# A hybrid-mixer encoder layer in one launch: the recurrence's places moved into the projections' input, its first stage moved ahead of the gated attention's last two heads

## The chip, the cores and the metric

The kernel runs on one core of a Trainium2 chip. The metric is the device time of one execution in microseconds (us). The engines are TensorE (PE, matrix products), VectorE (DVE), ScalarE (ACT), GpSimd (POOL) and SyncE (SP, which only starts DMAs here). Each engine works through its own list of instructions in a fixed order; semaphores hold an instruction back until what it needs is there. "Clock" is the TensorE clock that the profile shows as granted, as a share of full speed.

## The reference, cut to what matters

One encoder layer runs over 768 tokens (a sequence of 512 and one of 256) of 1,024 channels: a hybrid mixer, cross attention to 256 memory rows per sequence, and a feed-forward network. Only the mixer and the key and value product of the memory rows are touched by the change.

```python
def hybrid_mixer(h, p):
    proj = h @ p['w_in']
    rw = centred_shift(proj[..., :R_COLS], p['mu_prev'], p['mu_next'])
    gl = proj[..., R_COLS:]
    mixed = jnp.concatenate([rwkv7_group(rw, p), gla_group(gl, p)], axis=-1)
    return mixed @ p['w_out']

# rwkv7_group: 8 heads of 64, once forward and once in reverse over the tokens
def step(S, inp):
    r_t, w_t, k_t, v_t, kk_t, a_t = inp
    sa = jnp.einsum('bhij,bhj->bhi', S, -kk_t)
    S = (S * w_t[:, :, None, :] + sa[..., None] * (kk_t * a_t)[:, :, None, :]
         + v_t[..., None] * k_t[:, :, None, :])
    return S, jnp.einsum('bhij,bhj->bhi', S, r_t)

# gla_group: 4 heads of gated linear attention in chunks of 64 tokens, both directions
# cross_attention: kv = rms_norm(mem) @ p['wkv_x']
```

## The kernel before, in words

Channels stand on the partitions and tokens on the free axis. A float32 product is made from two rounded halves of each operand (hi and lo) in three matmuls, so a weight tile is loaded, rounded on ACT (`whi`) and its remainder taken on POOL or DVE (`wlo`).

**Projections.** `hT_hi` and `hT_lo` (pool `hp`) hold the normalised input. `blocks([(g, i), ...])` runs projection blocks of 128 columns each: g 0 to 3 are the gated attention's q/k, gate, value and decay columns, g 4, 5 and 6 are the columns r, k and v of the recurrence's head pairs 1, 2 and 3. Their matmuls write `pd` and read `hT_hi` and `hT_lo`.

**The recurrence** handles four pairs of heads, p = 0 to 3. For a pair, `begin(p)` makes decays and products of them on DVE and POOL, and `lower` multiplies them into chunk matrices on PE, which go out by DMA; `invert(p)` reads them back and inverts 96 triangles of 32x32 in a loop of 31 pairs of DVE operations (tiles `stmp`, `sqf`, `snf`); `joined(p)` reads the result by DMA and merges the triangles into 64x64 on PE (tiles `merge`, two passes of 48 matmuls each). The state is then carried over the chunks of 64 tokens by `step`: a chain PE, ACT, PE, ACT, PE, DVE for each pair of chunks, in `stage(q)`. A stage advances up to three independent jobs: the second half of pair q-1's long sequence, and both the first half of it and the short sequence for pair q. What a step reads stands in six "places" of 10 KB a partition (`pl`), filled by `products` from DRAM and PE. `finish` normalises a pair's result.

**The gated attention** runs head by head, `gla_head(h)`, in one arena of 13 x 768 floats (39 KB a partition) in pool `gp`, and ends with a multiply and a DMA to `mixd`.

**The memory rows.** `memory()` loads and splits the normalised memory rows into `mem_hi` and `mem_lo` (32 KB a partition together), and `memory_block(mem, b)`, 16 of them with 48 matmuls of 128x256 each, makes the keys and values. These blocks depend on nothing of the recurrence, so the scheduler lays them between the stages' small matmuls. Then `out_projection` (tiles `po`) multiplies the mixed result by `w_out`, whose hi and lo planes are loaded into tiles that are free by then.

**What sets the order.** The functions are called in program order; `tc.high_priority(offset=...)` draws steps (4000), products (3000), preparation and inversion (2000) and joins (6000) ahead of the calls around them. A scheduler then fixes each engine's list. Space is the other thing: a tile that takes another's place can be written only when the last reader of the old one is done. Around the change the calls before are

```python
        joined(1)
        blocks([(5, i) for i in range(3)])
        gla_head(2)
        blocks([(3, 3), (2, 3)])
        begin(2)
        invert(2)
        gla_head(3)          # pool gp closes; the places open in its space
```

and after these `prods(0, ...)`, `blocks([(6, i) ...])`, `stage(0)`; pool `hp` closes, `memory()` opens in new space, then `begin(3)`, `joined(2)`, `invert(3)`, the 16 memory blocks and stages 1 to 4.

Of the kernel before, what the change touches and what calls it, by code (L numbers as in the profile page):

```python
# [8 lines left out]
F32 = mybir.dt.float32  # L9
F32R = mybir.dt.float32r  # L10
# [6 lines left out]
P = 128  # L17
# [15 lines left out]
def kernel(ctx: ExitStack, tc: tile.TileContext, I, y_prompt, y_sample):  # L33
# [28 lines left out]
    cp = ctx.enter_context(tc.tile_pool(name="cp", bufs=1, reuse_waits="tile"))  # L62
    hp_cm = tc.tile_pool(name="hp", bufs=1, side="right", reuse_waits="tile")
    hp = hp_cm.__enter__()
    wp_cm = tc.tile_pool(name="wp", bufs=2, reuse_waits="tile")
    wp = wp_cm.__enter__()
    dp = ctx.enter_context(tc.tile_pool(name="dp", bufs=1, space=DRAM))
# [377 lines left out]

    def rkv_early(p, i):

        ot = hp.tile([P, T], F32, tag="gd", bufs=2, name="gd")
        rkv_block(p, i, lambda c, n: ot[:, c:c + n])
        dma(rkvd[p, i], ot)  # L450
        if i == 2:
            vt = tokens_first(ot)
            for h, hs in enumerate(HS):
                for par, ps_ in enumerate(HS):
                    dma(vtd[p][h][:, :, par * 64:par * 64 + 64], vt[ps_, :, hs])

    def tokens_first(ot):

        vt = hp.tile([P, T], F32, tag="gd", bufs=2, name="gd")
        for c, n in SEQS:  # L460
            pt = psd("gvt")
            for j in range(0, n, P):
                pe.transpose(out=pt[:, j:j + P], in_=ot[:, c + j:c + j + P], identity=ident)
            with tc.high_priority():
                dve.tensor_copy(out=vt[:, c:c + n], in_=pt[:, 0:n])
        return vt.rearrange("p (j e) -> p j e", e=P)

    def gla_dense(g, i):

        c0 = (1952, 2208, 2992, 2464)[g] + i * P  # L470
        w = load_block([(w_cols(c0, P), 0)], P)
        ot = hp.tile([P, T], F32, tag="gd", bufs=2, name="gd")
# [130 lines left out]

    mp_cm = tc.tile_pool(name="mp", bufs=1, reuse_waits="tile")
    mp = mp_cm.__enter__()
    tts, tdz = [], []
    for d in range(2):
        t = mp.tile([P, NCH, 64], F32, tag=f"tt{d}", name=f"tt{d}")
        pool.memset(t, 0.0)
        tts.append(t)  # L610
        tdz.append(mp.tile([P, NCH, 32], F32, name=f"tdz{d}"))
    px = mp.tile([P, NCH, 66], F32, tag="px", name="px")
    pool.memset(px, 1.0)
    px_at = px[:, :, 1:65]
# [199 lines left out]
    joined(0)  # L814


    with tc.tile_pool(name="gp", bufs=1, reuse_waits="tile") as gp:
        ones_f = gp.tile([P, P], F32, name="ones_f")
        dve.memset(ones_f, 1.0)
        arena = gp.tile([P, 13 * T], F32, name="arena")  # L820
# [119 lines left out]
        blocks([(0, 1), (1, 1), (3, 2), (2, 2)])  # L940
        joined(1)
        blocks([(5, i) for i in range(3)])
        gla_head(2)
        blocks([(3, 3), (2, 3)])
        begin(2)
        invert(2)
        gla_head(3)


    places = {}  # L950

    def open_places(pool_, gs):
        for g in gs:
            t = pool_.tile([P, 2560], F32, tag=f"pl{g}", name=f"pl{g}")
            places[g] = (t[:, 0:512].rearrange("p (h u x) -> p h u x", h=2, x=64),
                         t[:, 512:1280].rearrange("p (u i x) -> p u i x", u=4, x=64),
                         t[:, 1280:1792].rearrange("p (u h x) -> p u h x", u=4, x=64),
                         t[:, 1792:2304].rearrange("p (u x) -> p u x", x=P),
                         t[:, 2304:2560].rearrange("p (u x) -> p u x", x=64))

    mq1_cm = tc.tile_pool(name="mq1", bufs=1, reuse_waits="tile")
    mq1 = mq1_cm.__enter__()
    open_places(mq1, (0, 4, 1, 5, 2))
    yas = [mq1.tile([P, T], F32, tag="ya0", name="ya0")]

    def bc2(ap):

# [39 lines left out]
    def step(st, x, j, pc):  # L1007
# [54 lines left out]
        else:  # L1062
            dve.tensor_tensor(out=o, in0=y1, in1=o, op=ALU.add)
            dve.tensor_tensor(out=o, in0=y2, in1=o, op=ALU.add)

    def finish(st, seqs=SEQS, tiles=None, mixed=None):

        p, pa = st["p"], st["ya"]
        pb, bon, gt = tiles or (mq2.tile([P, T], F32, tag="fb", name="fb"),) * 3
        a, b = seqs[0][0], seqs[-1][0] + seqs[-1][1]  # L1070
        a, b = min(a, seqs[-1][0]), max(b, seqs[0][0] + seqs[0][1])
        cs = slice(a, b)
# [77 lines left out]
                prods(q + 1, (j // 2, 4 + j // 2))  # L1150

    prods(0, (0, 4, 1, 5))
    blocks([(6, i) for i in range(3)])
    stage(0)
    prods(0, (2,))
    hp_cm.__exit__(None, None, None)
    mq2_cm = tc.tile_pool(name="mq2", bufs=1, reuse_waits="tile")
    mq2 = mq2_cm.__enter__()
    open_places(mq2, (3,))
    yas += [mq2.tile([P, T], F32, name=f"ya{i}") for i in (1, 2)]  # L1160
    prods(0, (3,))
    mem = memory()
    begin(3)
    joined(2)
    invert(3)
    for b in range(16):
        memory_block(mem, b)
    stage(1)
    with tc.high_priority(offset=2000):
        finish(sts[0])  # L1170
# [16 lines left out]
    tiles = (mq2.tile([P, T], F32, tag="fb", name="fb"), *mo)  # L1187
# [5 lines left out]
    mq2_cm.__exit__(None, None, None)  # L1193
    hp_cm = tc.tile_pool(name="hp2", bufs=1, side="right", reuse_waits="tile")
    hp = hp_cm.__enter__()
    for k in order:
        if k != 3:
            load_split(mixd[k], *mix[k], lo_eng=pool)
    planes = []
# [8 lines left out]
    planes += [t[:, i, :] for i in range(5)]  # L1208
    wt = {}
    for i, k in enumerate(order):  # L1210
        pl = planes[4 * i:4 * i + 4]
# [77 lines left out]
    with tc.tile_pool(name="op1", bufs=1, reuse_waits="tile") as op1:  # L1289
        g_pre = gain_row(op1, "g_x_pre")  # L1290

        xn = [[op1.tile([P, 512], F32, name="xn")], [t[:, 512:T] for t in mo]]
        mo = [t[:, 0:512] for t in mo]

        def rows():
            return ((rk.tile([P, T], F32, tag="k", name="res0")[:, 0:512], mq1.tile([P, T], F32, tag="ya0", name="res1")[:, 0:512]), mo, xn)

        hT_hi, hT_lo = out_projection(op1, wt, mix, x_rows, rows, g_post, x1d, g_pre)
    mq1_cm.__exit__(None, None, None)
    mp_cm.__exit__(None, None, None)  # L1300
    rk_cm.__exit__(None, None, None)

# [440 lines left out]
```

## Time and profile before

| what | us |
|---|---|
| runs (median; lowest and highest of 3) | 1591.46; 1590.47 to 1599.93 |
| the profiled execution | 1596.87 |
| its span in the profile | 1595.0 |
| PE busy in it | 1442.8 (90%) |
| DVE busy in it | 1049.7 (66%) |
| ACT, POOL busy in it | 718.9, 514.6 |
| mean granted clock | 0.914 |

The profiled execution lies 1.87 us above its span and 5.41 above the median of the runs. Times in the profile count from the start of the span. From 0 to 289 us lie the first projections and the pairs 0 and 1 up to pair 0's join; from 289 to 893 all that the change moves; from 893 on cross attention and the feed-forward network, which it leaves as they are. [...]

### The profile page before, as it was taken

The page shows a single profiled execution, that of the slowest core. Times are in us where ns is not written, and L with a number is a line of the kernel's source. Part 1 is how long each engine was busy: PE and PEld are TensorE (multiplying, and loading weights), DVE is VectorE, ACT ScalarE, POOL GpSimd, SP SyncE. Part 2 cuts the span into 40 slices and gives each one's busy share as a digit, 9 for nine tenths or more (in the row PEclk, how much of TensorE's full clock was granted, in tenths as well). Part 3 has the DMA queues.
Part 4 walks back from the last instruction along what each step waited for, and adds up shares of the span by engine and source line. Part 5 has one row for each costly group of instructions (what it writes and reads, how often), then busy time and mean ns, then how long its engine had stood idle before and what let it go on. Part 6 is the DMA issues. An engine that isn't in the chain of part 4 may idle for free. (4 is left out here: it accounts for less than half of the span.)

```text
span 1595.0 us, 28271 instructions
## 1 busy us (share of the span) xinstructions
PE 1442.8 (90%) x10614; PEld 1246.0 (78%) x10614; DVE 1049.7 (66%) x1605; ACT 718.9 (45%) x1417; POOL 514.6 (32%) x576
## 2 busy tenths in 40 slices
PE   7999689889887889899888999996999999999996
PEld 6887578777775777778767888786999999787785
DVE  5545885497577795764455434448876676878886
ACT  5754344443333332333344354434555556544442
POOL 6416643494317342211531354420000001231223
PEclk9999798989875988888979999997999999999998
DMA  6686555556468447754452333235555447564434
GB/s 168 181 302 188 167 137 131 145 146 192 111 205 229 127 149 176 205 134 135 126 166 99 119 95 105 73 111 160 172 169 176 158 145 284 171 204 132 143 100 142
DMA packets 279565, 250.35 MB, mean 157 GB/s; under 512 B 89264, under 2 KB 227059, under 8 KB 279428
## 3 DMA queue, kind: packets, MB, share of 16 engines
q1 hardware_dynamic: 279428, 248.54, 52.1%
q8 instruction: 84, 1.38, 0.4%
q14 instruction: 53, 0.43, 0.1%
HBM read 164.11 MB, written 82.58 MB: 155 GB/s over the span
## 5 line engine op out<-in xcount | busy, mean ns | idle before, releaser
L148 POOL TENSOR_TENSOR wlo<-wraw,whi 128x256 fp32r<-128x256 f32 x192 | 176.8, 934 | 331.0 <-ACT whi L147 231.1
L247 PE MATMUL pd<-hT_hi,whi 128*128 128x256 f32 (+1 forms) x512 | 182.0, 356 | 12.6 <-DVE gd L325 8.2
L247 PE MATMUL pd<-hT_hi,wlo 128*128 128x512 f32 (+1 forms) x512 | 180.1, 354 | 4.0 <-POOL wlo L148 4.0
L247 PE MATMUL pd<-hT_lo,whi 128*128 128x256 f32 (+1 forms) x512 | 178.6, 350 | 0.3 <-DVE hT_lo L206 0.3
L1511 POOL TENSOR_TENSOR wl<-w,wh 128x1024 fp32r<-128x1024 f32 x8 | 21.2, 2649 | 329.8 <-ACT wh L1510 329.8
L247 PEld LDWEIGHTS pd<-hT_hi,whi 128*128 128x128 f32 x512 | 100.4, 196 | 27.6 <-issue 5.5
L247 PEld LDWEIGHTS pd<-hT_hi,wlo 128*128 128x128 f32 x512 | 99.6, 195 | 18.6 <-POOL wlo L148 5.3
L147 ACT ACTIVATE whi<-wraw 128x256 fp32r<-128x256 f32 x192 | 77.3, 414 | 78.2 <-PE pd L1104 22.9
L247 PEld LDWEIGHTS pd<-hT_lo,whi 128*128 128x128 f32 x512 | 100.4, 196 | 13.0 <-DVE hT_lo L206 0.5
L148 DVE TENSOR_TENSOR ul<-ur,uh 128x768 fp32r<-128x768 f32 x56 | 77.4, 1388 | 30.7 <-ACT uh L147 17.7
L147 ACT ACTIVATE uh<-ur 128x768 fp32r<-128x768 f32 x56 | 47.4, 847 | 107.8 <-PE gz L1520 52.0
L1510 ACT ACTIVATE wh<-w 128x1024 fp32r<-128x1024 f32 x64 | 67.1, 1053 | 35.9 <-PE fz L1520 24.2
L1520 PE MATMUL gx<-wh,uh 128*128 128x512 f32 x192 | 75.0, 397 | 4.3 <-DVE acc L1713 4.3
L1511 DVE TENSOR_TENSOR wl<-w,wh 128x1024 fp32r<-128x1024 f32 x56 | 68.2, 1219 | 15.1 <-ACT wh L1510 14.5
L1520 PE MATMUL gx<-wl,uh 128*128 128x512 f32 x192 | 75.9, 395 | 0.0
L1520 PE MATMUL gx<-wh,ul 128*128 128x512 f32 x192 | 75.4, 395 | 0.0
L1520 PE MATMUL fz<-hh,wh 128*128 128x384 f32 x192 | 66.0, 344 | 1.9 <-ACT wh L1510 1.9
L1511 POOL TENSOR_TENSOR wl<-ws,wh 128x1024 fp32r<-128x1024 f32 x16 | 40.6, 2536 | 79.6 <-ACT wh L1510 79.6
L1520 PE MATMUL fz<-hh,wl 128*128 128x384 f32 x192 | 65.2, 344 | 0.8 <-DVE wl L1511 0.8
L1520 PE MATMUL fz<-hl,wh 128*128 128x384 f32 x192 | 65.8, 343 | 0.0
L1510 ACT ACTIVATE wh<-ws 128x1024 fp32r<-128x1024 f32 x48 | 50.5, 1052 | 26.8 <-PE fx L1520 22.3
L1104 PE MATMUL pd<-mem_hi,whi 128*128 128x256 f32 x256 | 59.3, 308 | 1.4 <-ACT mo L1116 1.4
(476 smaller groups left out, 4306.9 us busy)
## 6 DMA issues: line engine op xcount, KB each, us to landing
w<-in_w_ff_dram SPq DMA_DIRECT2D x64, 512.0 KB
ur<-ud SPq DMA_DIRECT2D x56, 384.0 KB
wraw<-in_w_in_dram SPq DMA_DIRECT2D x108, 128.0 KB
ud<-u SPq DMA_DIRECT2D x32, 384.0 KB
ud<-us SPq DMA_DIRECT2D x24, 384.0 KB
wraw<-in_wkv_x_dram SPq DMA_DIRECT2D x64, 128.0 KB
lora<-lo_t SPq DMA_DIRECT2D x20, 384.0 KB
bkg<-bkd SPq DMA_DIRECT2D x24, 256.0 KB
```

The lines of the kernel that those rows point to most:

```text
L147: act.activation(out=hi, in_=src, func=AF.Copy)
L148: (lo_eng or pool).tensor_tensor(out=lo, in0=src, in1=hi, op=ALU.subtract)
L247: pe.matmul(out=out, lhsT=a, rhs=b, start=(i == 0), stop=(i == n - 1))
L1104: prev = order_after(pe.matmul(out=pd[:, c0:c0 + 256], lhsT=x, rhs=y[:, c0:c0 + 256], start=(k + i + c0 == 0), stop=(k + i + c0 == KD + 25 ...
L1510: act.activation(out=hi, in_=t[name], func=AF.Copy)
L1511: lo_eng.tensor_tensor(out=lo, in0=t[name], in1=hi, op=ALU.subtract)
L1520: pe.matmul(out=out, lhsT=a, rhs=b, start=first and i == 0, stop=last and i == n - 1, skip_group_check=True)
```

## The change

The two buffers `gd` get a pool of their own (`gdp`), which is used again later for two of the results `ya`, and for `xn` and `res1`. The two `tdz` become halves of one tagged tile. Pool `gp` with the arena stays open until after `gla_head(3)`, and four of the six places, with most of a fifth, take the space of `hT_hi` and `hT_lo`, so they can open as soon as the last projection block has read those. All projection blocks now come first, then stage 0, then heads 2 and 3 of the gated attention with the preparation and inversion of pair 2. `mem_hi` and `mem_lo` take the arena's space. Of the planes for `w_out`, 18 take the space of `mem_hi` and `mem_lo` after the last memory block. Nothing is computed that wasn't before, and nothing less.

```diff
-        ot = hp.tile([P, T], F32, tag="gd", bufs=2, name="gd")
+        ot = gdp.tile([P, T], F32, tag="gd", bufs=2, name="gd")
...
-    with tc.tile_pool(name="gp", bufs=1, reuse_waits="tile") as gp:
+    gp_cm = tc.tile_pool(name="gp", bufs=1, reuse_waits="tile")
+    gp = gp_cm.__enter__()
...
         joined(1)
         blocks([(5, i) for i in range(3)])
-        gla_head(2)
         blocks([(3, 3), (2, 3)])
-        begin(2)
-        invert(2)
-        gla_head(3)
+        blocks([(6, i) for i in range(3)])
...
-    mq1_cm = tc.tile_pool(name="mq1", bufs=1, reuse_waits="tile")
+    mq1_cm = tc.tile_pool(name="mq1", bufs=1, side="right", reuse_waits="tile")
     mq1 = mq1_cm.__enter__()
-    open_places(mq1, (0, 4, 1, 5, 2))
-    yas = [mq1.tile([P, T], F32, tag="ya0", name="ya0")]
...
+    plh, pll = (hp.tile([P, KD * T], F32, tag=n, name="pl_" + n) for n in ("hh", "hl"))
+    for t, gs in ((plh, (0, 4)), (pll, (1, 5))):
+        for i, g in enumerate(gs):
+            whole_place(g, t[:, 2560 * i:2560 * i + 2560])
+    place(3, plh[:, 5120:5632], pll[:, 5120:5888], mq1.tile([P, 512], F32, tag="pl3", name="pl3"), plh[:, 5632:6144],
+          pll[:, 5888:6144])
+    whole_place(2, mq1.tile([P, 2560], F32, tag="pl2", name="pl2"))
+    yas = [gdp.tile([P, T], F32, tag="gd", bufs=2, name=f"ya{i}") for i in range(2)]
...
     prods(0, (0, 4, 1, 5))
-    blocks([(6, i) for i in range(3)])
     stage(0)
-    prods(0, (2,))
-    hp_cm.__exit__(None, None, None)
+    prods(0, (2, 3))
+    gla_head(2)
+    begin(2)
+    invert(2)
+    gla_head(3)
+    gp_cm.__exit__(None, None, None)
     mq2_cm = tc.tile_pool(name="mq2", bufs=1, reuse_waits="tile")
     mq2 = mq2_cm.__enter__()
-    open_places(mq2, (3,))
-    yas += [mq2.tile([P, T], F32, name=f"ya{i}") for i in (1, 2)]
-    prods(0, (3,))
     mem = memory()
     begin(3)
     joined(2)
     invert(3)
+    yas.append(mp.tile([P, T], F32, tag="kds", name="ya2"))
     for b in range(16):
         memory_block(mem, b)
+    mq2_cm.__exit__(None, None, None)
     stage(1)
...
+    wo1_cm = tc.tile_pool(name="wo1", bufs=1, reuse_waits="tile")
+    wo1 = wo1_cm.__enter__()
+    planes = [wo1.tile([P, 512], F32R, name=f"w_out{i}") for i in range(18)]
     for n in ("snf", "sqf"):
         t = mp.tile([P, 2, 512], F32R, tag=n, name="w_" + n)
         planes += [t[:, 0, :], t[:, 1, :]]
-    for g in (0, 4, 1, 5):
-        t = mq1.tile([P, 5, 512], F32R, tag=f"pl{g}", name=f"w_pl{g}")
-        planes += [t[:, i, :] for i in range(5)]
+    planes.append(mp.tile([P, T], F32R, tag="tdz", name="w_tdz")[:, 0:512])
```

How the engines' lists move shows in three places. First, the end of the gated attention. On PE before, head 3's last matmuls (`gsum`) stand among the projection blocks (`pd<-hT`):

```order
L247 MATMUL pd<-hT_hi,wlo 128x256
L247 MATMUL pd<-hT_hi,whi 128x256
L921 MATMUL gsum<-arena,ones_f 128x512
L921 MATMUL gsum<-arena,ones_f 128x256
L247 MATMUL pd<-hT_lo,whi 128x256
L247 MATMUL pd<-hT_hi,wlo 128x256
L247 MATMUL pd<-hT_hi,whi 128x256
```

On PE after, they stand behind the last merges of pair 2 and among steps of stage 1 (`rec`); no projection block is left there:

```order
L918 MATMUL go<-arena 128x64 x2
L920 MATMUL go<-arena 128x128
L803 MATMUL merge_5696<-tt_1482,sqf 32x32 x24
L1032 MATMUL rec<-pl_4232 64x64 x4
L1040 MATMUL rec<-rh,pl_4232 64x64 x4
L1027 MATMUL rec<-pl_hh 64x64 x8
L926 MATMUL gsum<-arena,ones_f 128x512
L926 MATMUL gsum<-arena,ones_f 128x256
L1047 MATMUL rec<-pl_4232 64x64 x4
```

Of the two heads' DVE work, what stood beside pair 1's preparation and inversion now stands beside pair 2's inversion and pair 3's preparation.

Second, the first memory block (`pd<-mem_hi`). On PE before, it stands among the products of stage 0 (`sca`, `scb`) and the chunk matrices of pair 2 (`low`), 349 matmuls behind the last projection matmul:

```order
L1049 MATMUL rec<-pl_4468 64x64 x4
L991 MATMUL sca<-pl_4467,bkg 64x64
L992 MATMUL scb<-pl_4467,bkg 64x64
L685 MATMUL low<-bk 64x64
L1104 MATMUL pd<-mem_hi,whi 128x256 x2
L1104 MATMUL pd<-mem_lo,whi 128x256 x2
L685 MATMUL low<-bk 64x64 x14
```

On PE after, it stands in the middle of stage 1, 829 matmuls behind the last projection matmul, and behind pair 2's join:

```order
L1040 MATMUL rec<-rh,pl_hh 64x64 x4
L1032 MATMUL rec<-pl_hh 64x64 x4
L1040 MATMUL rec<-rh,pl_hh 64x64 x4
L1058 MATMUL rec<-pl_4232 64x64 x4
L1116 MATMUL pd<-mem_hi,whi 128x256 x2
L1116 MATMUL pd<-mem_lo,whi 128x256 x2
L1047 MATMUL rec<-pl_hh 64x64 x8
```

All of stage 0, two of four rounds of steps of stage 1, both heads of the gated attention, and pair 2's chunk matrices and join now come before any memory block.

Third, the end of the stages. On PE before, no memory matmul is left when the last steps run, and the output projection (`po`) follows them:

```order
L631 MATMUL hsum<-fb,ones_bd 128x256
L1018 MATMUL rec<-pl_5344 64x64 x4
L1023 MATMUL rec<-pl_5344 64x64 x4
L1031 MATMUL rec<-rh,pl_5344 64x64 x4
L1038 MATMUL rec<-pl_5344 64x64 x4
L1049 MATMUL rec<-pl_5344 64x64 x4
L247 MATMUL po<-w_snf,mix_bk 128x512 x2
```

On PE after, 264 memory matmuls stand between the last step and the output projection. Their beginning:

```order
L1116 MATMUL pd<-mem_hi,wlo 128x256 x2
L1058 MATMUL rec<-pl_hh 64x64 x4
L1125 MATMUL kvt<-ident,mo 128x128 x4
L1116 MATMUL pd<-mem_hi,whi 128x256 x2
L1116 MATMUL pd<-mem_lo,whi 128x256 x2
```

More of the change, by code (lines that the diff above doesn't have):

```diff
@@ L64 @@
     hp = hp_cm.__enter__()
+    gdp_cm = tc.tile_pool(name="gdp", bufs=1, side="right", reuse_waits="tile")
+    gdp = gdp_cm.__enter__()
     wp_cm = tc.tile_pool(name="wp", bufs=2, reuse_waits="tile")
@@ L457, in tokens_first @@
     def tokens_first(ot):
-        vt = hp.tile([P, T], F32, tag="gd", bufs=2, name="gd")
+        vt = gdp.tile([P, T], F32, tag="gd", bufs=2, name="gd")
         for c, n in SEQS:
@@ L471, in gla_dense @@
         w = load_block([(w_cols(c0, P), 0)], P)
-        ot = hp.tile([P, T], F32, tag="gd", bufs=2, name="gd")
+        ot = gdp.tile([P, T], F32, tag="gd", bufs=2, name="gd")
         for c, n, pd in channels_product(w, P, hT_hi, hT_lo):
@@ L605 @@
     mp = mp_cm.__enter__()
-    tts, tdz = [], []
+    tdz = mp.tile([P, 2, NCH, 32], F32, tag="tdz", name="tdz")
+    tdz = [tdz[:, d] for d in range(2)]
+    tts = []
     for d in range(2):
@@ L610 @@
         tts.append(t)
-        tdz.append(mp.tile([P, NCH, 32], F32, name=f"tdz{d}"))
     px = mp.tile([P, NCH, 66], F32, tag="px", name="px")
@@ L814 @@
     joined(0)
-    with tc.tile_pool(name="gp", bufs=1, reuse_waits="tile") as gp:
+    gp_cm = tc.tile_pool(name="gp", bufs=1, reuse_waits="tile")
+    gp = gp_cm.__enter__()
+    if True:
         ones_f = gp.tile([P, P], F32, name="ones_f")
@@ L942, with place, whole_place @@
         blocks([(5, i) for i in range(3)])
-        gla_head(2)
         blocks([(3, 3), (2, 3)])
-        begin(2)
-        invert(2)
-        gla_head(3)
+        blocks([(6, i) for i in range(3)])
     places = {}
[L952 to L959, printed above, removed]
-    mq1_cm = tc.tile_pool(name="mq1", bufs=1, reuse_waits="tile")
-    mq1 = mq1_cm.__enter__()
-    open_places(mq1, (0, 4, 1, 5, 2))
-    yas = [mq1.tile([P, T], F32, tag="ya0", name="ya0")]
+    mq1_cm = tc.tile_pool(name="mq1", bufs=1, side="right", reuse_waits="tile")
+    mq1 = mq1_cm.__enter__()
+    def place(g, xv, a_, bkt, rbk, tp):
+        places[g] = (xv.rearrange("p (h u x) -> p h u x", h=2, x=64), a_.rearrange("p (u i x) -> p u i x", u=4, x=64),
+                     bkt.rearrange("p (u h x) -> p u h x", u=4, x=64), rbk.rearrange("p (u x) -> p u x", x=P),
+                     tp.rearrange("p (u x) -> p u x", x=64))
+    def whole_place(g, t):
+        place(g, *(t[:, a:b] for a, b in ((0, 512), (512, 1280), (1280, 1792), (1792, 2304), (2304, 2560))))
+    plh, pll = (hp.tile([P, KD * T], F32, tag=n, name="pl_" + n) for n in ("hh", "hl"))
[6 more added lines that the diff above has]
+    yas = [gdp.tile([P, T], F32, tag="gd", bufs=2, name=f"ya{i}") for i in range(2)]
     def bc2(ap):
@@ L1064, in step, with finish_tile @@
             dve.tensor_tensor(out=o, in0=y2, in1=o, op=ALU.add)
+    def finish_tile():
+        return mp.tile([P, D], F32, tag="sxf", name="fb")[:, 0:T]
     def finish(st, seqs=SEQS, tiles=None, mixed=None):
         p, pa = st["p"], st["ya"]
-        pb, bon, gt = tiles or (mq2.tile([P, T], F32, tag="fb", name="fb"),) * 3
+        pb, bon, gt = tiles or (finish_tile(),) * 3
         a, b = seqs[0][0], seqs[-1][0] + seqs[-1][1]
@@ L1186 @@
     mo = [mp.tile([P, T], F32, tag="lsb", bufs=4, name="mo") for _ in range(2)]
-    tiles = (mq2.tile([P, T], F32, tag="fb", name="fb"), *mo)
+    tiles = (finish_tile(), *mo)
     with tc.high_priority(offset=2000):
@@ L1192 @@
         finish(sts[3], SEQS[:1], tiles, mix[3])
-    mq2_cm.__exit__(None, None, None)
-    hp_cm = tc.tile_pool(name="hp2", bufs=1, side="right", reuse_waits="tile")
-    hp = hp_cm.__enter__()
     for k in order:
@@ L1198 @@
             load_split(mixd[k], *mix[k], lo_eng=pool)
-    planes = []
+    wo1_cm = tc.tile_pool(name="wo1", bufs=1, reuse_waits="tile")
+    wo1 = wo1_cm.__enter__()
+    planes = [wo1.tile([P, 512], F32R, name=f"w_out{i}") for i in range(18)]
     for n in ("snf", "sqf"):
@@ L1208 @@
     planes += [t[:, i, :] for i in range(5)]
+    planes.append(mq1.tile([P, 512], F32R, tag="pl3", name="w_pl3"))
     wt = {}
@@ L1290 @@
         g_pre = gain_row(op1, "g_x_pre")
-        xn = [[op1.tile([P, 512], F32, name="xn")], [t[:, 512:T] for t in mo]]
+        xn = [[gdp.tile([P, T], F32, tag="gd", bufs=2, name="xn")[:, 0:512]], [t[:, 512:T] for t in mo]]
         mo = [t[:, 0:512] for t in mo]
         def rows():
-            return ((rk.tile([P, T], F32, tag="k", name="res0")[:, 0:512], mq1.tile([P, T], F32, tag="ya0", name="res1")[:, 0:512]), mo, xn)
+            return ((rk.tile([P, T], F32, tag="k", name="res0")[:, 0:512], gdp.tile([P, T], F32, tag="gd", bufs=2, name="res1")[:, 0:512]), mo, xn)
         hT_hi, hT_lo = out_projection(op1, wt, mix, x_rows, rows, g_post, x1d, g_pre)
+    wo1_cm.__exit__(None, None, None)
     mq1_cm.__exit__(None, None, None)
+    gdp_cm.__exit__(None, None, None)
     mp_cm.__exit__(None, None, None)
```

## The prediction

> **What bounds the kernel now.** I read the page, then the windows view (busy time of each engine between two moments), and last the instructions of single tiles and lines. The page:
>
> ```profile
> span 1595.0 us, 28271 instructions
> PE 1442.8 (90%) x10614; PEld 1246.0 (78%) x10614; DVE 1049.7 (66%) x1605; ACT 718.9 (45%) x1417; POOL 514.6 (32%) x576
> ```
>
> PE is the busiest engine on average, but the change touches only a part, cut here at events that the rows further down give: pair 0's join (289), last projection matmul (442), first memory matmul (503), end of pair 2's inversion (607) and of its join (rounded up to 646), last memory matmul (790), last step (826), end of the output projection (rounded to 894). Columns: stretch, length, then busy time of PE, weight load, DVE, ACT and POOL, the granted clock, DMA share and GB/s.
>
> ```profile
> 289.00:442.00 153.00, 136.00 (x1007) 114.96 (x1006) 109.43 (x142) 64.39 (x116) 80.29 (x68) 0.88 0.56 152
> 442.00:503.00 61.00, 46.27 (x649) 37.57 (x648) 46.74 (x87) 24.34 (x68) 24.04 (x22) 0.67 0.75 215
> 503.00:607.00 104.00, 89.35 (x1086) 76.34 (x1087) 87.03 (x182) 33.88 (x92) 49.55 (x41) 0.80 0.55 155
> 607.00:646.00 39.00, 37.55 (x561) 32.30 (x558) 15.92 (x34) 13.02 (x33) 7.29 (x10) 0.97 0.84 200
> 646.00:703.00 57.00, 48.81 (x659) 42.21 (x650) 50.55 (x141) 21.04 (x59) 11.40 (x15) 0.91 0.58 160
> 703.00:790.00 87.00, 84.85 (x1137) 72.58 (x1137) 35.71 (x96) 34.46 (x93) 22.53 (x35) 0.86 0.46 126
> 790.00:826.00 36.00, 25.30 (x178) 18.26 (x178) 24.85 (x56) 17.34 (x48) 16.09 (x26) 0.72 0.64 194
> 826.00:894.00 68.00, 63.58 (x290) 50.66 (x291) 33.12 (x56) 23.60 (x62) 12.13 (x24) 0.97 0.31 100
> ```
>
> Two things are to be seen. Where PE has filler it is nearly full (607 to 646: 37.55 of 39, clock 0.97); where it has only the recurrence's small matmuls (442 to 503) it is busy 46.27 of 61 at a clock of 0.67. And where PE is not full, DVE is: 87.03 of 104 between 503 and 607. PE's work in full-clock microseconds is busy time by clock, row by row: 119.7 + 31.0 + 71.5 + 36.4 + 44.4 + 73.0 + 18.2 + 61.7 = 456. The change keeps these 456 and DVE's work, so the question is only how the pieces cover one another.
>
> **The change, piece by piece.** I follow three stretches: A to the last projection matmul, B to the first memory matmul, C to the output projection.
>
> ```profile
> 289.00:442.00 153.00, 31.18 (x236) 27.22 (x236) 31.11 (x22) 32.87 (x45) 11.31 (x14) 0.88 0.56 152
> L247 PE MATMUL pd<-hT_hi,wlo x144: 274/389/792, 305.7 to 442.2; 128*128 128x512 f32 x72, 128*128 128x256 f32 x72
> L744 DVE TENSOR_TENSOR stmp<-sqf,snf x31: 192/387/925, 377.6 to 415.7; 112x31 f32<-112x31 f32 x2, 112x60 f32<-112x60 f32 x2, 112x87 f32<-112x87 f32 x2, 112x112 f32<-112x112 f32 x2
> L788 PE MATMUL merge<-tdz,lsb x96: 191/191/212, 430.2 to 436.3; 32*32 32x32 f32 x96
> L904 DVE TENSOR_TENSOR_SCAN arena<-arena x2: 3703/3703/3703, 334.4 to 405.8; 64x1536 f32<-64x1536 f32 x2
> L903 DVE TENSOR_TENSOR_SCAN arena<-arena x2: 3350/3390/3431, 331.0 to 402.5; 64x1536 f32<-64x1536 f32 x2
> ```
>
> *A.* The first row is the arena's share of 289 to 442: heads 2 and 3 leave with up to 31.1 us on DVE and 31.2 on PE. Pair 1's join (430.2) stands in PE's list before the last projection matmuls (442.2), 12 us dense, so PE's surplus gives nothing until the join comes earlier. What delays it for certain is in the inversion's loop (377.6 to 415.7): head 3's two scans of 3.4 and 3.7 us, and two multiplications, some 9.5 us. If every DVE microsecond of the heads lay on that chain it would be 31. POOL is busy 80.29 of 153, and pair 1's preparation there stays. I take 10: A ends at 432 instead of 442 (bounds 411 and 442).
>
> ```profile
> L744 DVE TENSOR_TENSOR stmp<-sqf,snf x31: 192/376/1642, 527.6 to 606.5; 112x31 f32<-112x31 f32 x2, 112x60 f32<-112x60 f32 x2, 112x87 f32<-112x87 f32 x2, 112x112 f32<-112x112 f32 x2
> 526.00:609.00 83.00, 76.79 (x165) 0.82 0.44 131
> L800 PE MATMUL merge<-tt,sqf x96: 191/191/212, 630.6 to 636.3; 32*32 32x32 f32 x96
> L1104 PE MATMUL pd<-mem_hi,whi x256: 274/281/581, 503.0 to 789.3; 128*128 128x256 f32 x128
> L147 ACT ACTIVATE mem_hi<-raw x16: 400/402/417, 484.9 to 501.9; 128x256 fp32r<-128x256 f32 x16
> L1019 ACT ACTIVATE rh<-rec x12: 271/278/296, 530.9 to 589.7; 128x128 f32<-128x128 f32 x12
> ```
>
> *B.* Memory tiles take the arena's space, so the first memory matmul waits for head 3's end, and in PE's list it stands behind pair 2's join. In before that chain ran from 442.2: inversion from 527.6 (85 us later) to 606.7, last merge at 636.3. Preparing pair 2 beside stage 0 is the same work as before; it starts a little before the last projection block now and memory's loads are gone from it, so 78 (bounds 66, the 85 less the DVE idle of 442 to 503, and 90). The inversion's 79 us were full of DVE work (second row, DVE alone: 76.79 of 83). Of that, half of stage 1's twelve steps leave (last row: all twelve lay between 530.9 and 589.7), and the two heads come in; leaving and coming nearly cancel at 79 (bounds 65, with every gap closed, and 105, with 31 us of the heads on top). The join's DMAs and merges keep 30. Then head 3's last multiply, its DMA out, and memory's load and split: the 16 splits took 17 us to the first matmul, begun early in part, so 14 (8 to 28). 432 + 78 + 79 + 30 + 14 = 633, where it was 503.0.
>
> Steps on PE now run beside the heads' matmuls and nothing dense. The waits that the change adds are memory's on the arena (SP's loads of the memory rows and their splits on ACT and POOL are queued behind it, then all 16 blocks) and `w_out`'s on the last memory block. The place loads' wait on `hT` costs one DMA trip, in the 78.
>
> ```profile
> L1019 ACT ACTIVATE rh<-rec x11: 270/278/278, 664.8 to 715.6; 128x128 f32<-128x128 f32 x11
> L1019 ACT ACTIVATE rh<-rec x8: 271/278/283, 745.2 to 777.5; 128x128 f32<-128x128 f32 x8
> L1019 ACT ACTIVATE rh<-rec x4: 259/278/278, 781.1 to 816.3; 128x128 f32<-128x128 f32 x4
> 787.42 0.40 PE L1104 MATMUL pd<-mem_hi,wlo 128*128 128x256 f32 x2
> 787.66 0.40 PE L1104 MATMUL pd<-mem_hi,whi 128*128 128x256 f32 x2
> 808.41 1.19 PE L247 MATMUL po<-w_snf,mix_bk 128*128 128x512 f32 x2 [1.29 <-POOL mix_px L148]
> 816.15 0.40 PE L247 MATMUL po<-w_snf,mix_bk 128*128 128x512 f32 x1
> 816.38 1.08 PE L247 MATMUL po<-w_pl,mix_bk 128*128 128x512 f32 x4
> 893.00 0.39 PE L247 MATMUL pd<-hT_hi,whi 128*128 128x512 f32 x1
> ```
>
> *C.* At 633 two rounds of stage 1, four each of stages 2 and 3, and stage 4 are left. One `rh` marks one step: 50.8 us for ten intervals, 32.3 for seven, so 4.6 to 5.1 a step and 14.5 a round of three: 145 for ten rounds. Stage 4 takes 45 (781.1 to 826). Then 264 memory matmuls, two of them each 0.24 us: 31. Sum 221, if the steps never wait for pair 3's join. The other way to reckon is PE: of the 456, A keeps 119.7 less 31.18 x 0.88, thus 92; B gets those 27, the 31 of stage 0, and an estimated 25 of the 108 between 503 and 646 (what its 365 memory matmuls, 43 us, leave is 65, and some two fifths of it, the join, half of stage 1 and pair 2's matrices, come ahead of memory), thus 83; the 288 output projection matmuls at 0.235 are 68. That leaves C 213. At the rate of 646 to 790, 117.4 in 144, it takes (213 - 31) / 0.815 + 31 = 254; at 0.97 it takes 220. I take 230, nearer the steps, since memory covers all of C: the output projection begins at 863, not 808.4.
>
> It took 84.6 (808.4 to 893.0) with the last steps inside; alone 68 / 0.97 = 70, and I add 8 for `w_out` planes that now load after the last memory block (0 to 20). 863 + 78 = 941 against 893.0: **48 us slower**. From the profiled execution, 1596.9 + 48 = 1645; it lay 5.4 above the runs' median, so on that scale 1639.
>
> **The clock.** The row of 442 to 503 has 0.67 where matmuls are sparse, and B is some 200 us of that kind. [...]
>
> **The rivals.**
> - *PE itself sets B.* [...] For it: 442 to 503 is already at 46 of 61 busy. Against it: pair 2's chain is mostly DVE and DMA. [...] Chance 0.14.
> - *Pair 2's inversion runs as pair 1's did.* The same 31 rounds took 38 us at 377.6, beside head 3. Then 41 less: 1598, no change. Against it: pair 3's preparation and both heads stand beside it. Chance 0.17.
> - *Faster: the heads fill DVE's gaps.* DVE's work from 289 to B's end is about 259 (109.43 + 46.74 + 87.03 + 15.92) less 15 for steps that move behind; my A and B give it 344 us, a share of 0.71. At 0.925, its share between 526 and 609, it takes 264, the first memory matmul comes at 560 in place of 633 with the splits, and the time is 1566. It decides from a share of 0.82 (296 us, break-even) and gives over 1% at 0.87. For it: nothing but DVE is full there. Against it: the join's trip (15.92 of 39 busy) and places' loads are DMA waits. Chance 0.13.
> - *The change does not do what it says*: the last projections end no earlier and stage 0 starts as before. Its sum is 10 more, 1649, within my case.
>
> **How the numbers follow.** My forecast has 0.56, 1639, by itself 1612 to 1670 (A's 10 either way, the inversion's 65 and C's 254). The range must reach the no-change case and leaves out the faster one and some large sums of upper bounds: 1588 to 1675. One per cent, 16 us, is what a measurement here can tell. Faster 0.13; same 0.18 (the second rival and a little); slower 0.69.
>
> **What would show it.** Right: last projection matmul near 432; no memory matmul before 615; clock below 0.7 in B; DVE's share from 289 to there near 0.7; a tail of memory matmuls of 31 us at full clock; the output projection from 850 to 880. Wrong: pair 2's inversion under 50 us, memory beginning before 580, or steps in C under 4.5 us apart.

## The result, and the profile after

The changed kernel takes 1696.81 us (median of 4 runs, 1693.43 to 1698.81) against 1593.98 us for the kernel before: a ratio of 1.0639, 95% interval 1.0598 to 1.0679. It is slower, as forecast, by about twice the forecast amount (some 102 us, where 48 had been reckoned), and it lies above the forecast range of 1588 to 1675.

The page of the changed kernel, its first lines:

```profile
span 1696.0 us, 28319 instructions
PE 1464.0 (86%) x10614; PEld 1260.7 (74%) x10614; DVE 1050.6 (62%) x1605; ACT 722.2 (43%) x1417; POOL 495.9 (29%) x576
```

PE, DVE, ACT and POOL run as many instructions as before, and their busy times differ by some 21 us at most; the span has grown by 101. The windows view shows where. The stretches are cut at the changed kernel's own events (columns as in the prediction: length, busy PE, weight load, DVE, ACT, POOL, granted clock, DMA share, GB/s).

```profile
291.50:432.00 140.50, 114.55 (x834) 95.56 (x834) 80.41 (x128) 39.90 (x82) 56.87 (x54) 0.90 0.61 162
432.00:523.00 91.00, 63.95 (x723) 50.89 (x720) 56.77 (x98) 21.38 (x56) 19.12 (x12) 0.55 0.61 163
523.00:600.00 77.00, 44.52 (x356) 35.28 (x356) 71.77 (x105) 26.88 (x42) 29.58 (x28) 0.52 0.29 88
600.00:632.00 32.00, 24.01 (x275) 21.11 (x278) 16.15 (x17) 10.46 (x18) 0.00 (x0) 0.50 0.65 136
632.00:660.00 28.00, 16.85 (x216) 13.47 (x213) 26.36 (x60) 14.28 (x41) 15.61 (x18) 0.56 0.42 119
660.00:707.00 47.00, 38.83 (x613) 32.86 (x617) 31.65 (x89) 12.94 (x39) 6.01 (x8) 0.64 0.48 111
707.00:858.00 151.00, 149.56 (x2012) 126.43 (x2003) 75.94 (x216) 64.67 (x183) 31.25 (x41) 1.00 0.44 130
858.00:890.00 32.00, 29.50 (x241) 28.12 (x240) 3.94 (x5) 12.90 (x27) 16.55 (x26) 1.00 0.46 141
890.00:1000.00 110.00, 82.40 (x375) 66.26 (x374) 50.08 (x87) 39.30 (x101) 32.47 (x61) 0.88 0.39 121
```

From 432 to 660 PE is busy 149 us of 228 at a clock of 0.50 to 0.56, some 80 us of full-clock work. From 707 to 858 it is full (149.56 of 151) at full clock (1.00). The memory matmuls, which ran from 503 on before, now begin at 660 and lie in the later stretch. The events, from the tile view of the changed kernel (first and last start of each group):

```profile
L249 PE MATMUL pd<-hT_hi,wlo x178: 274/390/793, 284.6 to 431.7; 128*128 128x256 f32 x90, 128*128 128x512 f32 x88
L749 DVE TENSOR_TENSOR sqf<-sqf,stmp x31: 192/375/1903, 523.2 to 599.4; 112x31 f32<-112x31 f32 x2, 112x60 f32<-112x60 f32 x2, 112x87 f32<-112x87 f32 x2, 112x112 f32<-112x112 f32 x2
L803 PE MATMUL merge<-tt,sqf x96: 236/236/258, 623.5 to 631.3; 32*32 32x32 f32 x96
L41 SPq DMA_DIRECT2D mixd<-arena x4: 332/379/433, 224.2 to 643.2; - x4
L150 POOL TENSOR_TENSOR mem_lo<-raw,mem_hi x16: 769/884/942, 646.2 to 658.7; 128x256 fp32r<-128x256 f32 x16
L1116 PE MATMUL pd<-mem_hi,whi x256: 276/281/683, 659.9 to 889.5; 128*128 128x256 f32 x128
L249 PE MATMUL po<-w_out,mix_bk x72: 387/394/793, 917.6 to 985.7; 128*128 128x512 f32 x72
990.99 0.39 PE L249 MATMUL pd<-hT_hi,whi 128*128 128x512 f32 x1
```

The projections end at 431.7 (442.2 before), pair 2's inversion runs from 523 to 599, its join ends at 631.3 (636.3 before), head 3's result is sent out of the arena at 643.2, memory is split on POOL until 658.7 and its first matmul comes at 659.9 (503.0 before). The last one is at 890, the output projection starts at 917.6 (808.4) and the next product at 991.0 (893.0). So 98 of the trace's 101 us lie ahead of this point.

Between 890 and 917.6 PE does next to nothing. The view of PE's waits, from 660 to 918:

```profile
PE po L249 <- POOL mix_px L150: 25.9, 1, 25.9
PE kvt L1125 <- ACT mo L1122: 4.7, 7, 0.9
```

### The profile page after: what moved, and what is told of

Read it like the earlier page. It is cut to its first block, busy times and chain, and to the rows that moved or that the text cites. A ratio compares the mean times of both kernels' runs of the same rounds, so it can differ in the third digit from the quotient of the medians.

```text
span 1696.0 us, 28319 instructions
## 1 busy us (share of the span) xinstructions
PE 1464.0 (86%) x10614; PEld 1260.7 (74%) x10614; DVE 1050.6 (62%) x1605; ACT 722.2 (43%) x1417; POOL 495.9 (29%) x576
## 5 line engine op out<-in xcount | busy, mean ns | idle before, releaser
L150 POOL TENSOR_TENSOR wlo<-wraw,whi 128x256 fp32r<-128x256 f32 x192 | 161.3, 852 | 347.1 <-ACT whi L149 225.5
L249 PE MATMUL pd<-hT_hi,wlo 128*128 128x256 f32 (+1 forms) x512 | 178.8, 351 | 2.3 <-POOL wlo L150 2.3
L1116 PE MATMUL pd<-mem_hi,wlo 128*128 128x256 f32 x256 | 57.9, 300 | 0.0
```

Source lines behind the costliest of these rows:

```text
L150: (lo_eng or pool).tensor_tensor(out=lo, in0=src, in1=hi, op=ALU.subtract)
L249: pe.matmul(out=out, lhsT=a, rhs=b, start=(i == 0), stop=(i == n - 1))
L1116: prev = order_after(pe.matmul(out=pd[:, c0:c0 + 256], lhsT=x, rhs=y[:, c0:c0 + 256], start=(k + i + c0 == 0), stop=(k + i + c0 == KD + 25 ...
```

## The experiments

Each run is given as a ratio to the kernel before on its own chip, and as microseconds of some 1590. The changed kernel stands at 1.0639 on this scale. The code cuts are shortened: `...` marks what is left out.

### Each delay alone, in the kernel before

The question was whether memory's late start costs, or the late steps. In the kernel before, the memory tiles can be made to wait: a small piece of pair 2's join result is copied into them and stored first.

```diff
-        hi, lo = (mq2.tile([P, KD, 512], F32R, name=n) for n in ("mem_hi", "mem_lo"))
+        hi, lo = (mq2.tile([P, KD, 512], F32R, tag=n, name=n) for n in ("mem_hi", "mem_lo"))
...
-    mem = memory()
     begin(3)
     joined(2)
+    late = dp.tile([2, 32, 32], F32, name="late")
+    for i, n in enumerate(("mem_hi", "mem_lo")):
+        t = mq2.tile([P, KD, 512], F32, tag=n, name="late_" + n)
+        act.activation(out=t[32:64, 0, 0:32], in_=tts[1][32:64, NCH - 1, 0:32], func=AF.Copy)
+        dma(late[i], t[32:64, 0, 0:32])
+    mem = memory()
     invert(3)
```

A first try copied a piece that the join never writes:

> The kernel before, with the memory tiles made to wait for pair 2's join: a 32x32 piece of the join's result is copied into them and stored first, so the first memory matmul comes near 655 and not at 503. Places, heads and stages stand as in before. Theory M (late cover is what costs): 43 us of memory matmuls that ran before 646 must run behind, where before had 44 us of room on PE between 646 and 826, so part of it fits: 1615 to 1645. Rival H (the heads beside pair 2's inversion and the late stage 1 cost it, memory's lateness is free): 1580 to 1600.

Its first memory matmul came at 515.7, so it delayed nothing of weight, and its 1590.55 us (ratio 1.0010, 0.9986 to 1.0034) decide nothing. With the piece as above:

> The kernel before, the memory tiles waiting for pair 2's join as was meant in the run before it: the piece copied is now one that the join writes last, so the first memory matmul comes near 655. Stages 0 and 1 stay where they were. Theory X (two ways lead to the output projection, the steps' chain and PE's work from the first memory matmul on; each had slack in before, the change is late on both): memory's way ends near 860, the loads behind it add up to 25: 1630 to 1665. Rival H (memory's lateness is free as long as the steps are on time): 1585 to 1605.

1657.64 us, ratio 1.0426 (1.0401 to 1.0451): 68 us. Its memory matmuls, its steps behind stage 0, and PE's wait ahead of the output projection:

```profile
L1104 PE MATMUL pd<-mem_hi,whi x256: 274/281/683, 640.7 to 854.6; 128*128 128x256 f32 x128
L1019 ACT ACTIVATE rh<-rec x40: 257/278/283, 518.1 to 801.5; 128x128 f32<-128x128 f32 x40
PE po L247 <- POOL mix_px L148: 24.7, 1, 24.7
```

The steps are done sooner than before (last `rh` at 801.5, 816.3 before). Memory ends at 854.6 in place of 789.3, and 24.7 us of waiting follow: the changed kernel's picture, with none of its places or its order. So late memory alone makes two thirds of the changed kernel's loss here. The steps' delay alone was made by putting three tiles into the turn of their PSUM banks:

```diff
     joined(2)
+    with tc.high_priority(offset=5000):
+        for i in range(3):
+            pt = psc("hold")
+            pe.matmul(out=pt[0:32, 0:32], lhsT=tts[1][32:64, NCH - 1, 0:32], rhs=tts[1][32:64, NCH - 1, 0:32],
+                      start=True, stop=True)
```

> The kernel before, with three one-matmul tiles on pair 2's join's result put into the turn of the steps' PSUM banks, so that stage 1 begins behind that join, near 640, and not at 531; memory stays where it was and fills PE meanwhile. Theory X: some forty steps at 5 us follow from 640, the last ends at 845 to 860 in place of 826: 1610 to 1635. Rival M (only memory's lateness costs): 1585 to 1600.

1596.89 us, ratio 1.0048 (1.0022 to 1.0075): 8 us. Its forty steps of stages 1 to 4:

```profile
L1019 ACT ACTIVATE rh<-rec x40: 258/277/286, 621.5 to 810.7; 128x128 f32<-128x128 f32 x40
```

Stage 1 is 91 us late (530.9 before), and the last step still comes at 810.7. The steps have that much room in this kernel: before, no step begins between 619.0 and 664.8, around pair 2's last merge (636.3), nor between 722.0 and 745.2, around pair 3's (729.9). Theory X's price for them (20 us or more) was wrong.

> The kernel before with both delays: stage 1 and the memory blocks behind pair 2's join, the places, the heads and the projections as in before. Theory X: this is the changed kernel's delay without its new places and order of heads, 1660 to 1705. If the heads beside pair 2's inversion or the places cost much by themselves: under 1640.

1662.68 us, ratio 1.0461 (1.0442 to 1.0482): memory's delay and hardly more, at the lower end of the expected range. Memory runs from 608.4 to 855.9 there, in the changed kernel from 659.9 to 889.5:

```profile
L1104 PE MATMUL pd<-mem_hi,whi x256: 274/280/683, 608.4 to 855.9; 128*128 128x256 f32 x128
```

### PE's work or the steps' chain

Here seven eighths of each memory block's matmuls are left out (42 of 48), in both kernels, with loads, splits, transposes and stores kept.

```diff
-        for k, (wh, wl) in enumerate(w):
+        for k, (wh, wl) in list(enumerate(w))[:1]:
...
-                        start=(k + i + c0 == 0), stop=(k + i + c0 == KD + 257)), prev)
+                        start=(k + i + c0 == 0), stop=(i + c0 == 258)), prev)
```

> The kernel before with one eighth of each memory block's matmuls (42 of 48 left out, with the loads, splits, transposes and stores kept): 80 us of PE's work at full clock are gone. If the recurrence's chain bounds it where memory was filler: 1560 to 1590. If PE bounds: 1515 to 1540.

> The changed kernel with the same seven eighths of the memory matmuls left out. Theory M: what separates the two kernels is memory's work standing behind, so without it they come within 45 us of each other: 1595 to 1630. Rival H: the distance stays near 95: 1650 to 1685.

The kernel before: 1589.62 us, ratio 0.9994 (0.9966 to 1.0022). Some 80 us of full-clock work are gone (busy time by clock, from 442 to 826: 271 before, 189 here) and nothing is saved. The changed kernel: 1637.67 us, ratio 1.0303 (1.0260 to 1.0345), some 53 us saved. The kernel before, first as it is and then without that work, between 640 and 826:

```profile
640.00:826.00 186.00, 164.48 (x2009) 137.71 (x2011) 113.43 (x295) 75.91 (x207) 52.16 (x78) 0.85 0.55 155
```

```profile
640.00:826.00 186.00, 141.65 (x1772) 109.67 (x1772) 112.72 (x300) 67.83 (x186) 37.15 (x58) 0.68 0.50 143
```

PE's busy share and its clock fall, and the time stays: in the kernel before the memory blocks' matmuls are free. The prediction had used the first row's kind as a rate at which PE gets through work. It is no such rate; PE idles there for want of work.

The changed kernel stays 48 us behind even without memory's work. Its steps are late there: the last one comes at 857.5, in the kernel before without that work at 817.0:

```profile
L1019 ACT ACTIVATE rh<-rec x48: 259/278/283, 443.0 to 817.0; 128x128 f32<-128x128 f32 x48
L1028 ACT ACTIVATE rh<-rec x48: 257/277/285, 440.8 to 857.5; 128x128 f32<-128x128 f32 x48
```

With memory's work it comes at 848.9 in the changed kernel, so these matmuls alone are not what makes the steps late. The 48 us were tried with the edit on the banks that follows below:

> The changed kernel with seven eighths of the memory matmuls left out (42 of 48 of each block) and heads 2 and 3 on the projections' PSUM banks, so that stage 1 is early again: both ways shortened. Theory X: the 48 us that the left-out work did not remove go with stage 1's lateness, 1585 to 1612. Rival: the time stays at 1625 to 1640, and something else holds the chain.

1622.38 us, ratio 1.0208 (1.0174 to 1.0241): 15 of the 48 go with stage 1's lateness. The last step still comes at 838.5; what holds the other 33 is open.

PE's clock was tested by itself, with 400 matmuls of 128x128 that nobody reads, called behind head 3:

> The changed kernel with 400 added 128x128 matmuls that nobody reads, called behind head 3, so that the scheduler lays them where PE is idle ahead of memory; they cost PE about 0.1 to 0.2 us each and keep its clock up. Theory K (PE's half clock is what makes that stretch long): the clock between 523 and 640 rises from 0.52 to over 0.8 and the first memory matmul comes before 645. Rival (DVE, POOL and DMA set it): the clock rises, the first memory matmul stays between 655 and 690.

1695.07 us, ratio 1.0664 (1.0621 to 1.0707), no gain, though the time includes the added matmuls themselves. The stretch from 523 to 640 in the changed kernel, and then in this one:

```profile
523.00:640.00 117.00, 73.98 (x692) 60.02 (x694) 95.07 (x140) 42.79 (x72) 31.39 (x29) 0.53 0.38 99
```

```profile
523.00:640.00 117.00, 97.39 (x978) 89.10 (x979) 92.89 (x136) 36.91 (x59) 30.67 (x28) 0.82 0.37 96
```

The clock rises from 0.53 to 0.82, and pair 2's last merge comes at 630.6 in place of 631.3:

```profile
L803 PE MATMUL merge<-tt,sqf x96: 190/191/213, 622.6 to 630.6; 32*32 32x32 f32 x96
L1116 PE MATMUL pd<-mem_hi,whi x256: 274/281/561, 696.6 to 889.8; 128*128 128x256 f32 x128
```

So PE's clock was not what held the stretch up to that join. The first memory matmul came at 696.6, later than either theory allowed, because the added matmuls stand ahead of it on PE until 696.5; behind 640 this run therefore says nothing about the clock. The last memory matmul comes where it came without them (889.8, 889.5).

### The wait ahead of the output projection

The mixed rows are loaded through the same buffers and the same queue as the memory blocks' weights, and come last there. In this run the last five blocks are called behind these loads.

```diff
-    for b in range(16):
+    for b in range(11):
         memory_block(mem, b)
-    mq2_cm.__exit__(None, None, None)
...
             load_split(mixd[k], *mix[k], lo_eng=pool)
+    for b in range(11, 16):
+        memory_block(mem, b)
+    mq2_cm.__exit__(None, None, None)
```

> The changed kernel with the last five memory blocks called behind the loads of the mixed rows, so that these stand ahead of the blocks' weight loads in SP's queue and in the turn of the raw buffers. Theory L (25.9 us of PE's idle time ahead of the output projection come from these loads standing behind the last blocks): that wait falls to under 10, the time to 1672 to 1685. Rival: the wait belongs to w_out's planes, which take memory's space after the last block: it stays above 18 and the time above 1688.

1688.61 us, ratio 1.0616 (1.0577 to 1.0655), which the intervals don't tell apart from the changed kernel and which lies above theory L's range. The wait fell to 4.1 us, as theory L says, but the last memory matmul went from 890 to 905: in the tail PE now waits for the blocks' own halves, 7.1 us on ACT and 3.4 on POOL. The wait had moved. Next, the mixed rows were split on ACT and DVE, not wholly on POOL (`lo_eng=dve` in place of `lo_eng=pool`), in both kernels:

> The changed kernel with the loads of the mixed rows split on ACT and DVE, not both halves on POOL. Theory P (the 25.9 us ahead of the output projection are POOL's: 21 pieces at 0.40 and 0.73 us are 24 us, which begin only as the last memory block's weights are split): the wait falls under 12, the time to 1675 to 1686. Rival Q (the queue: the loads are issued only from 880 to 909): the wait stays over 18, the time over 1688.

> The kernel before with the same split on ACT and DVE. There these pieces lie beside the last steps. Theory P: nothing to gain, 1585 to 1596, since they were ready when the steps were. If DVE's share of them delays the last steps: up to 1605.

The changed kernel: 1681.63 us, ratio 1.0569 (1.0542 to 1.0596), some 11 us better. Its wait:

```profile
PE po L249 <- ACT w_out L149: 12.5, 1, 12.5
```

Half of the 25.9 us was POOL's. The other half, 12.5, is for `w_out`, as the prediction had it at 8. The kernel before: ratio 1.0001 (0.9986 to 1.0016), nothing; there the 21 loads are issued from 768 to 803, beside the last steps, and not from 880 to 909.

### In the changed kernel itself

Stage 1 begins at 627 there. The heads' `go` tiles use the steps' PSUM banks and are called ahead of it. With heads 2 and 3 on the projections' banks:

```diff
...
+    psy_[0] = psd
     gla_head(2)
     begin(2)
     invert(2)
     gla_head(3)
+    psy_[0] = psc
```

> The changed kernel with heads 2 and 3 writing to the PSUM banks of the projections, not to those of the steps. Theory S (stage 1 begins at 616 and not at 531 because its banks come behind head 3's in their turn): stage 1 begins before 560 and is done before the first memory matmul; as PE is full from 707 to 858, what moves ahead of 660 shortens that stretch by its work, 15 to 25: 1672 to 1682. Rival D (ahead of 660 DVE is the bound): the steps' DVE work lengthens the way to the first memory matmul by as much as they save: 1690 to 1702.

> Both of the two edits before together. If each removes its own loss: 1648 to 1665. If one hides the other: no better than the better of the two.

The first: 1685.97 us, ratio 1.0595 (1.0567 to 1.0623); together with the loads ahead: 1683.45 us, 1.0583 (1.0542 to 1.0624). In the first, stage 1 begins at 534.5, the first memory matmul slips from 659.9 to 683.4 and the last goes from 889.5 to 881.9:

```profile
L1031 ACT ACTIVATE rh<-rec x40: 257/277/285, 534.5 to 848.5; 128x128 f32<-128x128 f32 x40
L1119 PE MATMUL pd<-mem_hi,whi x256: 274/281/682, 683.4 to 881.9; 128*128 128x256 f32 x128
```

So the banks were what held stage 1, and both theories had half of the rest: the time lies between their ranges. The two edits together are not told apart from the bank edit alone. Then the heads: left out of both kernels but for their loads and their store, so that the arena is free at once.

```diff
+            if h > 1:
+                dma(mixd[4 + h], qs)
+                return
             e1 = slot_(8)
```

> The changed kernel with heads 2 and 3 of the gated attention left out but for their loads and store, so that the arena is free early and the order is otherwise the changed one. Theory X (memory's start behind the heads is what costs): the first memory matmul comes before 510 and the time is 1560 to 1600, within 25 us of the kernel before with the same left out. Rival (places, planes or stage order cost by themselves): 40 us or more above that.

> The kernel before with heads 2 and 3 left out in the same way, as the measure for the run before: the heads lay beside projections there, and pair 1's inversion gets 10 to 30 us of DVE back: 1560 to 1585.

The changed kernel so: 1575.64 us, ratio 0.9896 (0.9861 to 0.9931). The kernel before so: 1582.43 us, 0.9932 (0.9910 to 0.9954). With the heads out of the way the changed kernel loses nothing, and memory begins at 454.4:

```profile
L1119 PE MATMUL pd<-mem_hi,whi x256: 274/281/682, 454.4 to 731.5; 128*128 128x256 f32 x128
```

So the places, the planes and the order of the rest don't cost the 102 us. What costs is the two heads between the recurrence and memory; this run takes out their work, their banks and their hold on the arena together and does not part them. Three orders that move them elsewhere, with the changed places. First the calls in the old order:

> The changed kernel with the calls in the old order: heads 2 and 3 and pair 2's preparation beside the projection blocks again, the places still where the projections' input was, memory still in the arena's space. Theory M (the loss is PE's missing cover: memory blocks begin at 660 instead of 503, and PE then works off the rest behind): the arena is free at head 3's end, near 430, so the first memory matmul comes at 470 to 505, none is left behind the last step, and the time is 1575 to 1605. Rival R (it is the places' new space and its loads that cost, not the order): 1650 or more.

1611.25 us, ratio 1.0109 (1.0071 to 1.0147). The last projection and the steps:

```profile
L249 PE MATMUL pd<-hT_hi,wlo x178: 274/392/682, 285.0 to 457.6; 128*128 128x256 f32 x90, 128*128 128x512 f32 x88
L1032 ACT ACTIVATE rh<-rec x48: 266/277/290, 474.9 to 824.6; 128x128 f32<-128x128 f32 x48
```

Memory begins at 485, earlier than before, and that is worth nothing. Stage 0 begins at 474.9 in place of 444.9, behind the last projection at 457.6, whose input the places take. Rival R's cause can hold for at most these 17 us; that the late stage 0 costs them was not tested. Next, the heads called among the projection blocks, head 2 right behind pair 1's join, pair 2's preparation behind stage 0:

> The changed kernel with heads 2 and 3 called among the projection blocks earlier than in the kernel before (head 2 right behind pair 1's join, head 3 behind pair 2's blocks) and pair 2's preparation behind stage 0 as changed. Theory X: memory begins by 500 and the time is 1580 to 1612. It beats the kernel before only if the last projection ends before 442, since the places wait for it.

1602.20 us, ratio 1.0065 (1.0042 to 1.0087), the best of the versions with the changed places and still no better than the kernel before; its last projection ends at 462.2 and its stage 0 begins at 476.9, later yet than in the run before it, at some 10 us in place of 17. Last, all projections first and the heads ahead of stage 0:

> The changed kernel with all projection blocks first, as changed, but heads 2 and 3 and pair 2's preparation called ahead of stage 0, so that the arena is free before memory is wanted. Theory X: memory begins by 500, no tail is left, the time is 1580 to 1610: nearly all of the change's loss is back with its places kept. If projections first is what costs: over 1630.

1645.82 us, ratio 1.0350 (1.0321 to 1.0378), well above theory X's range and above the 1630 that was set for the case that projections first costs by itself. Against that case stands the run without the heads, which has all projections first and loses nothing. Memory begins early, and yet:

```profile
L1116 PE MATMUL pd<-mem_hi,whi x256: 274/282/682, 505.7 to 843.8; 128*128 128x256 f32 x128
L1028 ACT ACTIVATE rh<-rec x48: 256/277/325, 474.5 to 840.2; 128x128 f32<-128x128 f32 x48
```

Pair 2's inversion begins at 550.6 (527.6 before) and the last step's `rh` comes at 840.2 (816.3), with a wait of 17.2 us for POOL's splits behind. An early start of memory does not suffice. That the heads' DVE work ahead of pair 2's preparation makes that difference is argued from the order, not shown.

## Why the prediction was right in direction and wrong in size

The step that failed is the price of memory's late start, at both of its ends: from pair 2's join to its first matmul it took 28.6 us where 14 had been forecast, and the loads and splits behind its last block were put at 8 us and took 25.9. The preparation of pair 2 was priced too low besides.

**A (to the last projection matmul)** was right as a number, 432 forecast and 431.7 measured, and partly by luck. The prediction hung A on pair 1's join, with 12 us of dense matmuls behind. The inversion and the join in the changed kernel:

```profile
L747 DVE TENSOR_TENSOR stmp<-sqf,snf x31: 184/359/984, 361.7 to 392.5; 112x31 f32<-112x31 f32 x2, 112x60 f32<-112x60 f32 x2, 112x87 f32<-112x87 f32 x2, 112x112 f32<-112x112 f32 x2
L791 PE MATMUL merge<-tdz,lsb x96: 191/224/258, 406.7 to 414.5; 32*32 32x32 f32 x96
```

The join came 23.5 us earlier (406.7, 430.2 before), and the projections ended 25 us behind it, not 12. The two misses nearly cancel to the forecast 10.

**B** was forecast to end at 633 and ended at 659.9. Of its steps, the inversion (79 forecast, 76.5 measured) and the join (30 and 32) were right. "Preparing pair 2 beside stage 0 is the same work as before ... so 78" failed: it took 91, more even than before's 85. I had taken 7 off without a row that held them. From the last chunk matrix matmul to the inversion it is 16 us in both kernels (507.0 to 523.2, 511.2 to 527.6), so the excess lies ahead of these matrices. Single DVE operations are slow there beside POOL's (up to 1.85 us, where 0.29 is the median, below), but DVE is busy no longer than before (56.8 us of 91, 59.7 of 85.6), so that alone does not explain it; the 13 us were not taken apart. "The 16 splits took 17 us to the first matmul, begun early in part, so 14" failed as well: none could begin before head 3's result had left the arena at 643.2, POOL then took 16 subtractions at 0.88, and with the heads' tail behind the join it came to 28.6.

**C** was right as a number, 230 forecast and 230 measured, and wrong as a reading: that the number fits is luck. The rate of 0.815 was taken from a stretch of the kernel before where PE had too little to do. In the changed kernel PE ran at 1.00 from 707 to 858, and memory's work was the bound: without it the output projection begins at 861.3, not 917.6. The steps' pace, reckoned beside it, gave 823 for the end of the steps, and their last `rh` came at 849. It is late without memory's matmuls as well (857.5), and with stage 1 early on the projections' banks (848.5), and still, though less, with both (838.5). So neither alone makes this miss, and its cause is open.

**The output projection** has the largest failed term: "I add 8 for `w_out` planes". The wait was 25.9 us. I looked at the planes that take memory's space and not at the mixed rows, whose 21 loads go through the memory blocks' buffers and queue. When memory runs last, they do too, and POOL splits them with nothing left beside it. Alone the projection took 73.4, where 70 was reckoned.

Summed up: 13 + 15 + 18 us from these three terms, and 3 for the projection's own length, turn the forecast 48 into 97 of the 98 of the trace.

**The rivals.** "PE itself sets B" falls, up to pair 2's join, with the run that raised the clock to 0.82: the join came 0.7 us earlier. The low clock was real: the granted clock in B was 0.50 to 0.56. What failed is the step from that clock to a longer B, which no run shows. "Pair 2's inversion runs as pair 1's did" fell: 76.5 us, not 38. The faster rival fell: DVE's share from 291.5 to 660 was 0.68 (251.5 of 368.5). Its 0.82 was never near.

**The range** went to 1675 and the kernel to 1697. Each failed term came out above its upper bound: 91 over 90 for the preparation, 28.6 over 28 for the splits, 25.9 over 20 for the wait. The three bounds together would have added 38 us, to 1677; I had left them out as "some large sums of upper bounds". The splits and the wait both hang on memory's late start, so they go high together; the preparation lies ahead of it. Some of the range's own figures don't come out of what they name: 85 less DVE's idle of 442 to 503 is 71, not 66; 79 less DVE's gaps of 526 to 609 is 73, not 65; and the three terms named for 1612 to 1670 give 1615 to 1673. None of these changes the outcome.

**What the runs settle.** Memory's lateness alone costs 68 us in the kernel before, the steps' lateness alone 8, both 73. The rest of the 102, some 29, stands beside memory starting 52 and ending 34 us later than in the run with both delays, behind head 3; that it comes from there is argued, not shown. The steps of the changed kernel are late as well, and 33 us of that, seen when memory's work is left out, stay open. Without the two heads the changed kernel is no slower than the kernel before without them.

## What to carry to other kernels

Filler work was free here as long as it ended before the work that it fills (a ratio of 0.9994 with seven eighths of its matmuls left out) and cost 68 us when it alone came late, so ask of a tile's space not only who frees it but what waits for the last of the filler: here loads through the same buffers and queue. An engine's rate in a stretch where it waits for others was no measure of how fast it would catch up (0.815 reckoned, busy 149.56 of 151 us at a clock of 1.00 in the changed kernel); leaving the filler's work out of both kernels showed in two runs which one it bounds. And terms that hang on one event should be moved together when a range is made, here the splits ahead of memory's blocks and the loads behind them.

## What was not expected of the hardware

Small DVE operations beside a POOL operation. An addition of 64x128 in the steps takes 0.29 us in the median and up to 1.85 us in the preparation of pair 2 (DVE's line from 432 to 660, what POOL ran at one time, and DVE's operations then):

```profile
L1055 DVE TENSOR_TENSOR pl_hl<-t,old x8: 283/290/1852, 470.5 to 500.5; 64x128 f32<-64x128 f32 x8
484.57 1.81 POOL L719 TENSOR_TENSOR kds<-kds,wc 128x768 f32<-128x768 f32 x1 [2.91 <-DVE wc L657]
486.46 1.80 POOL L667 TENSOR_TENSOR bk<-wb,wa 64x768 f32<-64x768 f32 x1
484.72 3.69 DVE L1055 TENSOR_TENSOR pl_hl<-t,old 64x128 f32<-64x128 f32 x2
```

Two of these additions, issued at 484.72, took 3.69 us together; the two POOL operations beside them took 1.81 and 1.80. In the kernel before the same addition took at most 0.71 us from 442 to 660. Such meetings are not new with the change. In the kernel before, an operation of pair 2's inversion (`stmp`, 112x87), issued at 601.19, took 1.64 us, where 0.376 is the median of its line; it ended at 602.83, and a POOL multiplication of 64x768 ran beside it from 600.15 to 602.73. The prediction showed the 1.64 as the maximum of that line, and nothing was made of it. Beside the same multiplication a DVE addition of 128x128, issued at 600.99, took 0.28 us. Whether, and why, one operation holds up the other is not shown here.
